# Two token halves of 320 and 320 columns in place of 256 and 384, in contiguous tiles of 640

## The chip, the cores and the metric

The kernel runs on one core of a Trainium2 chip. The metric is the time of one execution on the device, in microseconds (us). The engines are TensorE (matmul; PE in the profile, its weight loads PEld), VectorE (DVE), ScalarE (ACT), GpSimd (POOL) and SyncE (SP, which only issues transfers here). They run side by side, each through its own list of instructions in order, and wait for each other through semaphores.

## The reference, cut to what matters

Two layers of a trunk that works on 640 tokens: 128 of a prompt and 512 of a sample, which have their own modulation vectors.

```python
def _layer(x, cvec, p, ctx):                     # once for the prompt, once for the sample
    sh1, sc1, g1, sh2, sc2, g2 = split(silu(cvec) @ p['ada_w'] + p['ada_b'], 6)
    h = rms(x, p['norm1_g']) * (1 + sc1) + sh1   # over the 1024 features of a token
    sc_b, sc_c, sc_h, q, k, v, dn_qkv, dn_z, dn_a, dn_b = split(h @ p['w_in'])
    y_sc = sc_b * dwconv(sc_c * sc_h)            # short gated convolution
    y_att = attention(q, k, v)                   # windowed, with a cached context for the sample
    y_dn = gated_delta(dn_qkv, dn_z, dn_a, dn_b) # forward and backward scan over chunks
    x = x + g1 * (concat([y_sc, y_att, y_dn]) @ p['w_out'])
    h2 = rms(x, p['norm2_g']) * (1 + sc2) + sh2
    return x + g2 * ((silu(h2 @ p['w_gate']) * (h2 @ p['w_up'])) @ p['w_down'])
```

All inputs are float32. The model has 1024 features (8 tiles of 128) and 2816 hidden ones (22 tiles).

## The kernel before, in words

Activations lie feature-major: a tile has 128 features as partitions and tokens as columns. So that the products keep float32's precision at the speed of the rounded type, every operand is split into a high part (rounded to float32r) and a low part (the exact rest), and a product of a k-tile is three matmuls: high weights by high activations, high by low, low by high (lines 200 to 206 in `fm_product`; weights `whi`, `wlo` are made from `raw` by `split`, lines 173 and 174).

One accumulator in PSUM holds at most 512 columns, so the 640 tokens are taken in two parts, called halves in the names. Before the change part 0 has tokens 0 to 255 (the prompt's 128 and the sample's first 128) and part 1 tokens 256 to 639. Each part of each feature tile is a tile of its own, high and low: `apool` has 16 slots under the tag `a0` (256 columns) and 16 under `a1` (384 columns). The normalised activations (`hhi`, `hlo`), then the mixer's output (`m0h`, `m0l`, `m1h`, `m1l` in the profile, by part), then the second norm's output and so on go through these slots in turn. A slot is given to the next tile when all reads of the tile in it are over. The feed-forward's hidden tiles (`act0h` and so on, tag `act`) are cut in the same way.

The program of a layer:

- `Norm`: for the residual `xt` (8 tiles of 640 tokens), the squares of a tile are added to `acc` by part (`add`, lines 355 to 361); the last tiles to be finished ("late": three of them after w_out, two after w_down) are squared apart (line 374). `stats` sums acc and the late squares over the partitions with matmuls against a column of ones, one column of PSUM per chunk of 128 tokens (lines 379, 381), makes the scale with VectorE (384) and GpSimd (386) and spreads it over the partitions with a matmul against the identity, per chunk (389). `high` scales a tile (VectorE, 418), adds the shift and rounds (ScalarE, 423 to 427), and makes the low part (VectorE, 431, or GpSimd, 425).
- `mixer`: the projections, the short convolution, the DeltaNet (Gram matrices, inverses of triangular blocks, scan) and the attention, in an order written out in `SEQ`. `make_mix` takes the tiles of the mixer's output; `split` and `put_out` fill them by blocks of tokens; `part_out` multiplies tiles 0, 1, 6 and 7 by w_out and adds to the residual.
- w_out for tiles 2 to 5 (`rows`): the last group has four feature tiles (4 to 7), all on part 0 first, then `half(0)` is asked for, then all four on part 1, then `half(1)`.
- Feed-forward in three chunks of hidden tiles. The first two hidden tiles (`lead`) take gate and up on part 0 first, high parts ahead of low ones, then on part 1; the others take gate 0, gate 1, up 0, up 1. w_down follows each chunk; in the first layer the last three feature tiles are again a group, part 0 before part 1, for the norm ahead of the second layer's mixer. There two leading projections read part 0 first.

The order of instructions on each engine is made by a planner when the kernel is built: it simulates the engines with durations of its own and takes what is ready, by program order and a few raised priorities (the weights' splits). TensorE's order therefore depends on when the planner thinks that inputs are ready, and one-column sums stand between products where there was room. Dependencies go by the region of a tile that is read or written; slots go by whole tiles.

## Time and profile before

| what | value |
|---|---|
| median of three runs | 1807.85 us (1805.13 to 1810.63) |
| span of the profiled execution | 1806.5 us, 34244 instructions |
| TensorE busy | 1725.5 us, 96%, 14179 matmuls |
| VectorE busy | 981.2 us, 54% |
| ScalarE busy | 636.2 us, 35% |
| GpSimd busy | 113.2 us, 6% |
| mean granted clock of TensorE | 0.975 of full speed |

The page gives the profiled execution by its span, from the first to the last instruction; the times of the runs hold what lies around it too. "Busy" of TensorE counts a matmul from its start to a modelled end, and matmuls overlap: how fast a stream runs is read from its starts. A row of the timeline has the start in us, the time that it took, the engine, the line, what is written from what, the shapes and the count of instructions merged into it; in brackets stands idle time just before it and what ended it. PEclk is the granted clock of TensorE as a share of 2.4 GHz; it has two levels, 0.5 (1.2 GHz) and 1.

### The profile page before, as it was taken

The page shows a single profiled execution, that of the slowest core. Times are in us where ns is not written, and L with a number is a line of the kernel's source. Part 1 is how long each engine was busy: PE and PEld are TensorE (multiplying, and loading weights), DVE is VectorE, ACT ScalarE, POOL GpSimd, SP SyncE. Part 2 cuts the span into 40 slices and gives each one's busy share as a digit, 9 for nine tenths or more (in the row PEclk, how much of TensorE's full clock was granted, in tenths as well). Part 3 has the DMA queues.
Part 4 walks back from the last instruction along what each step waited for, and adds up shares of the span by engine and source line. Part 5 has one row for each costly group of instructions (what it writes and reads, how often), then busy time and mean ns, then how long its engine had stood idle before and what let it go on. Part 6 is the DMA issues. An engine that isn't in the chain of part 4 may idle for free. (4 is left out here: it accounts for less than half of the span.)

```text
span 1806.5 us, 34244 instructions
## 1 busy us (share of the span) xinstructions
PE 1725.5 (96%) x14179; PEld 1566.9 (87%) x14179; DVE 981.2 (54%) x2324; ACT 636.2 (35%) x1330; POOL 113.2 (6%) x230
## 2 busy tenths in 40 slices
PE   5998999999999999999999879999999999999998
PEld 3887875488999999999988879655899999999998
DVE  3799767666433333333477995777563333333333
ACT  3545244544322122212255442556352212221221
POOL 1111112000000000000012011220010000000000
PEclk7999999999999999999999989999999999999999
DMA  8512234656242222222232222455722222222222
GB/s 287 174 48 68 80 105 126 204 165 227 70 134 78 82 71 80 73 72 78 91 106 72 60 60 77 144 150 161 231 59 71 71 82 70 82 71 73 80 66 75
DMA packets 230025, 188.41 MB, mean 104 GB/s; under 512 B 11566, under 2 KB 206062, under 8 KB 229870
## 3 DMA queue, kind: packets, MB, share of 16 engines
q1 hardware_dynamic: 212992, 170.70, 31.4%
q10 hardware_dynamic: 16878, 15.53, 2.7%
q8 instruction: 111, 1.82, 0.4%
q14 instruction: 44, 0.36, 0.1%
HBM read 168.64 MB, written 17.56 MB: 103 GB/s over the span
## 5 line engine op out<-in xcount | busy, mean ns | idle before, releaser
L173 ACT CAST whi<-raw 128x1024 fp32r<-128x1024 f32 (+2 forms) x191 | 190.2, 996 | 598.9 <-PE pmm L202 271.5
L174 DVE TENSOR_TENSOR wlo<-raw,whi 128x1024 fp32r<-128x1024 f32 (+2 forms) x191 | 220.9, 1158 | 224.3 <-ACT whi L173 223.1
L200 PE MATMUL pmm<-hhi,whi 128*128 128x256 f32 x1008 | 319.0, 317 | 6.6 <-ACT dnp L517 5.3
L203 PE MATMUL pmm<-hhi,wlo 128*128 128x256 f32 x1008 | 317.4, 316 | 7.1 <-DVE wlo L174 7.1
L202 PE MATMUL pmm<-hlo,whi 128*128 128x256 f32 x960 | 301.7, 314 | 0.0
L200 PE MATMUL pmx<-hhi,whi 128*128 128x384 f32 (+1 forms) x688 | 213.0, 310 | 1.0 <-ACT hhi L427 0.7
L203 PE MATMUL pmx<-hhi,wlo 128*128 128x384 f32 (+1 forms) x688 | 212.9, 310 | 0.0
L200 PEld LDWEIGHTS pmm<-hhi,whi 128*128 128x128 f32 x1008 | 195.9, 194 | 11.1 <-ACT dnp L517 6.1
L203 PEld LDWEIGHTS pmm<-hhi,wlo 128*128 128x128 f32 x1008 | 195.7, 194 | 8.4 <-DVE wlo L174 7.7
L202 PE MATMUL pmx<-hlo,whi 128*128 128x256 f32 (+1 forms) x640 | 197.6, 309 | 0.0
L202 PEld LDWEIGHTS pmm<-hlo,whi 128*128 128x128 f32 x960 | 185.7, 193 | 0.7 <-issue 0.4
L200 PEld LDWEIGHTS pmx<-hhi,whi 128*128 128x128 f32 x688 | 130.3, 189 | 2.5 <-ACT hhi L427 1.5
L203 PEld LDWEIGHTS pmx<-hhi,wlo 128*128 128x128 f32 x688 | 130.3, 189 | 0.4 <-issue 0.4
L202 PEld LDWEIGHTS pmx<-hlo,whi 128*128 128x128 f32 x640 | 121.3, 190 | 0.0
L1533 DVE SCALAR_TENSOR_TENSOR av<-sg,pmx 128x256 f32<-128x256 f32 (+1 forms) x88 | 42.9, 488 | 131.8 <-PE pmx L203 123.9
L446 DVE SCALAR_TENSOR_TENSOR xt<-pmx,mod,xt 128x128 f32<-128x128 f32 (+1 forms) x96 | 39.1, 436 | 96.2 <-PE pmx L203 96.0
L446 DVE SCALAR_TENSOR_TENSOR xt<-pmm,mod,xt 128x128 f32<-128x128 f32 (+1 forms) x96 | 39.0, 436 | 91.6 <-PE pmm L203 89.1
L492 PE MATMUL pmm<-wlo,hhi 128*128 128x256 f32 x240 | 69.2, 289 | 0.7 <-DVE wlo L174 0.7
L491 PE MATMUL pmm<-whi,hhi 128*128 128x256 f32 x240 | 69.7, 292 | 0.0
L493 PE MATMUL pmm<-whi,hlo 128*128 128x256 f32 x240 | 69.3, 289 | 0.0
L1524 ACT ACTIVATE th<-pmm 128x256 f32<-128x256 f32 (+1 forms) x88 | 38.2, 434 | 76.7 <-PE pmm L203 70.7
L1526 DVE SCALAR_TENSOR_TENSOR sg<-th,pmm 128x256 f32<-128x256 f32 (+1 forms) x88 | 42.6, 485 | 41.1 <-ACT th L1524 41.1
(450 smaller groups left out, 3798.0 us busy)
## 6 DMA issues: line engine op xcount, KB each, us to landing
adaw<-in_ada_w_dram SPq DMA_DIRECT2D x64, 512.0 KB, 3.9
raw<-in_w_gate_dram SPq DMA_DIRECT2D x44, 512.0 KB, 3.9
raw<-in_w_up_dram SPq DMA_DIRECT2D x44, 512.0 KB, 3.9
raw<-in_w_in_dram SPq DMA_DIRECT2D x36, 512.0 KB, 4.8
araw<-in_ada_w_dram SPq DMA_DIRECT2D x32, 512.0 KB, 5.0
raw<-in_w_down_dram SPq DMA_DIRECT2D x32, 512.0 KB, 4.1
raw<-in_w_down_dram SPq DMA_DIRECT2D x16, 384.0 KB, 3.6
xm<-xscr SPq DMA_DIRECT2D x16, 320.0 KB, 4.9
```

The source lines that it names most:

```text
L173: (hi_eng or A.copy)(hi, src)
L174: (lo_eng or V).tensor_tensor(out=lo, in0=src, in1=hi.bitcast(F32), op=ALU.subtract)
L200: mm(o, lhsT=wh[:, k], rhs=ah, start=k == 0, stop=False)
L202: mm(o, lhsT=wh[:, k], rhs=al, start=False, stop=False)
L203: mm(o, lhsT=wl[:, k], rhs=ah, start=False, stop=not lead and k == n - 1)
L446: V.scalar_tensor_tensor(out=x[:, sl], in0=pt[:, a0:a1], scalar=gate[:, g:g + 1], in1=x[:, sl], op0=ALU.mult, op1=ALU.add)
L491: mm(pt, lhsT=ah[:, ts], rhs=wh[:, k % 4], start=k == 0, stop=False)
L492: mm(pt, lhsT=ah[:, ts], rhs=wl[:, k % 4], start=False, stop=False)
L493: mm(pt, lhsT=al[:, ts], rhs=wh[:, k % 4], start=False, stop=k == 7)
L1524: A.activation(th, pg[:, 0:n], AF.Tanh, scale=0.5)
L1526: V.scalar_tensor_tensor(out=sgs[h], in0=th, scalar=1.0, in1=pg[:, 0:n], op0=ALU.add, op1=ALU.mult)
L1533: V.scalar_tensor_tensor(out=av, in0=sgs[h], scalar=0.5, in1=pu[:, 0:n], op0=ALU.mult, op1=ALU.mult)
```

## The change

The border between the parts moves from token 256 to token 320, so both have 320 columns, and it no longer lies on a multiple of 128. High and low parts become one tile of 640 columns each (class `Act`, tag `a`, 16 slots), of which a part is a slice. What follows from this in the code: products, gate, up and residual pieces have 320 columns (part 0's residual goes in pieces of 128 and 192 columns, since the prompt ends at 128); `Norm.add` squares part by part; `stats` takes its sums in four chunks of 80 tokens per part, and spreads them in four; at the start of the kernel, where the sums come from token-major rows of 128, the border cuts the third block, so three chunks per part. Writers of whole blocks of tokens no longer cut at the border. The rest of the diff takes comments away.

```diff
-HB = ((0, 256), (256, 640))      # the two parts of the tokens that one product takes
-HN = (256, 384)
+HB = ((0, 320), (320, 640))
+HH = 320
...
-    def atiles(pool, tag, name):
-        return tuple(tuple(pool.tile([128, HN[h]], F32R, tag=f"{tag}{h}", name=f"{name}{h}{x}", bufs=16) for x in "hl")
-                     for h in range(2))
+    class Act:
+        def __init__(self, pool, tag, name, bufs=16):
+            self.hi, self.lo = (pool.tile([128, TOK], F32R, tag=tag, name=f"{name}{x}", bufs=bufs) for x in "hl")
+        def __getitem__(self, h):
+            return self.hi[:, HB[h][0]:HB[h][1]], self.lo[:, HB[h][0]:HB[h][1]]
...
-        o = pt[:, 0:HN[h]]
+        o = pt[:, 0:HH]
...
-            a0, a1 = HB[parts[0]][0], HB[parts[-1]][1]
-            sq = self.ft(a1 - a0, "sq")
-            A.activation(sq, self.xt[k][:, a0:a1], AF.Square)
             for h in parts:
-                V.tensor_tensor(out=self.acc[h], in0=self.acc[h], in1=sq[:, HB[h][0] - a0:HB[h][1] - a0], op=ALU.add)
+                sq = self.ft(HH, "sq")
+                A.activation(sq, self.xt[k][:, HB[h][0]:HB[h][1]], AF.Square)
+                V.tensor_tensor(out=self.acc[h], in0=self.acc[h], in1=sq, op=ALU.add)
...
+            if sums is None:
+                chunks = [(0, 80, t, t * 80) for t in range(4)]
+            elif h == 0:
+                chunks = [(0, 128, 0, 0), (0, 128, 1, 128), (0, 64, 2, 256)]
+            else:
+                chunks = [(64, 128, 0, 0), (0, 128, 1, 64), (0, 128, 2, 192)]
...
-                for t in range(nt):
-                    ts = slice(t * 128, (t + 1) * 128)
-                    mm(st[:, t:t + 1], lhsT=self.acc[h][:, ts], rhs=ones_c, start=True, stop=False)
+                for _, p1, t, a0 in chunks:
+                    ts = slice(a0, a0 + p1)
+                    mm(st[0:p1, t:t + 1], lhsT=self.acc[h][:, ts], rhs=ones_c, start=True, stop=False)
                     for sq in sqs:
-                        mm(st[:, t:t + 1], lhsT=sq[:, ts], rhs=ones_c, start=False, stop=sq is sqs[-1])
-                sums = st[:, 0:nt]
+                        mm(st[0:p1, t:t + 1], lhsT=sq[:, ts], rhs=ones_c, start=False, stop=sq is sqs[-1])
+                sums = st[0:np_, 0:nt]
...
-            for t in range(nt):
-                mm(self.bc[h][:, t * 128:(t + 1) * 128], lhsT=y2[:, t:t + 1].to_broadcast([128, 128]), rhs=ident,
-                   start=True, stop=True)
+            for p0, p1, t, a0 in chunks:
+                mm(self.bc[h][:, a0:a0 + p1 - p0], lhsT=y2[p0:p1, t:t + 1].to_broadcast([p1 - p0, 128]),
+                   rhs=ident[p0:p1, p0:p1], start=True, stop=True)
...
-            hi, lo = (apool.tile([128, n], F32R, tag=f"a{h}", name=name) for name in ("hhi", "hlo"))
-            self.out[k][h] = (hi, lo)
+            if self.out[k] is None:
+                self.out[k] = Act(apool, "a", "h")
+            hi, lo = self.out[k][h]
...
-            return ((0, 128, 0), (128, 256, 128))
-        return ((0, 384, 256),)
+            return ((0, 128, 0), (128, HH, 128))
+        return ((0, HH, HH),)
...
+            cs = slice(t0 * 128, (t0 + nt) * 128)
             for hp in range(2):
-                for h, cs, ts in spans(t0 * 128, (t0 + nt) * 128):
-                    hi, lo = mix[6 + hp][h]
-                    split(po[:, hp, ts], hi[:, cs], lo[:, cs])
+                split(po[:, hp, 0:nt * 128], mix[6 + hp].hi[:, cs], mix[6 + hp].lo[:, cs])
...
-                mix[k] = atiles(apool, "a", "m")
+                mix[k] = Act(apool, "a", "m")
             for m in range(2):
-                for h in range(2):
-                    split(ysc[m][:, HB[h][0]:HB[h][1]], mix[m][h][0], mix[m][h][1])
+                split(ysc[m], mix[m].hi, mix[m].lo)
...
             for tag, bufs in (("th", 3), ("sg", SG_BUFS), ("av", 3)):
-                fp.tile([128, HN[1]], F32, tag=tag, name=tag, bufs=bufs)
+                fp.tile([128, HH], F32, tag=tag, name=tag, bufs=bufs)
...
-                    act.append(atiles(fp, "act", "act"))
+                    act.append(Act(fp, "act", "act"))
```

## Rows read from the trace of the kernel before

**Rows 1.** The page: busy us (share of the span), and PEclk in 40 slices.

```profile
PE 1725.5 (96%) x14179; PEld 1566.9 (87%) x14179; DVE 981.2 (54%) x2324; ACT 636.2 (35%) x1330; POOL 113.2 (6%) x230
...
PEclk7999999999999999999999989999999999999999
```

**Rows 2.** Busy us by stretch: length, PE, PEld, DVE, ACT, POOL, PEclk, DMA, GB/s.

```profile
1000.00:1100.00 100.00, 90.29 (x970) 84.19 (x969) 87.83 (x213) 41.62 (x85) 8.13 (x26) 0.91 0.23 67
...
1600.00:1700.00 100.00, 100.00 (x683) 100.00 (x682) 35.62 (x57) 19.48 (x26) 0.00 (x0) 1.00 0.27 78
```

**Rows 3.** Who PE waited for: us in total, times, longest.

```profile
PE pdn L301 <- DMA araw<-in_ada_w_dram: 8.0, 10, 3.4
...
PE pmm L200 <- ACT dnp L517: 5.3, 2, 3.0
```

**Rows 4.** Line 200 alone over the whole span: PE and PEld busy (count).

```profile
0.00:1806.50 1806.50, 849.06 (x2720) 520.21 (x2720) 0.98 0.35 104
```

**Rows 5.** Timeline of PE: streams of 272, 256 and 384 columns, first and last.

```profile
945.89 0.29 PE L491 MATMUL pmm<-zw,hhi 128*128 128x272 f32 x1
...
948.80 0.29 PE L493 MATMUL pmm<-zw,hlo 128*128 128x272 f32 x1
...
1305.89 0.28 PE L200 MATMUL pmm<-m0h,whi 128*128 128x256 f32 x1
...
1308.76 0.28 PE L200 MATMUL pmm<-m0h,whi 128*128 128x256 f32 x1
...
1318.50 0.33 PE L200 MATMUL pmm<-m1h,whi 128*128 128x384 f32 x1
...
1322.66 0.28 PE L200 MATMUL pmm<-hhi,xhi 128*128 128x256 f32 x1
```

**Rows 6.** One-column sums: a burst's start and end; weight loads of 32 and 128 columns.

```profile
1331.45 0.36 PE L379 MATMUL pxo<-ones_c,acc 128*128 128x1 f32 x2
...
1333.24 0.73 PE L206 MATMUL pmx<-hlo,whi 128*128 128x256 f32 x4
...
L278 PEld LDWEIGHTS pdn<-adaw,c 128*32 128x32 f32 x512 | 13.6, 109 | 18.5 <-DMA adaw<-in_ada_w_dram 8.1 <-issue 5.7
...
L381 PEld LDWEIGHTS pxo<-ones_c,sq x80: 186/192/295, 429.1 to 1333.1; 128*128 128x128 f32 x80
```

**Rows 7.** Spreading the scales, line 389: both halves in the timeline; the whole line.

```profile
1316.02 0.71 PE L389 MATMUL pkq<-ident,ny 128*128 128x128 f32 x4
1316.48 0.42 PE L202 MATMUL pmx<-m1l,whi 128*128 128x384 f32 x1
...
1334.56 1.49 PE L389 MATMUL pkq<-ident,ny 128*128 128x128 f32 x6 [0.24 <-POOL ny L386]
...
L389 PE MATMUL pkq<-ident,ny x40: 274/421/582, 13.8 to 1335.6; 128*128 128x128 f32 x40
```

**Rows 8.** Timeline around the second layer's feed-forward start: scaling, and PE's waits.

```profile
1316.76 2.16 DVE L418 SCALAR_TENSOR_TENSOR t<-xt,msc,pkq 128x128 f32<-128x128 f32 x8 [0.21 <-PE pkq L389]
...
1322.25 0.34 DVE L418 SCALAR_TENSOR_TENSOR t<-xt,msc,pkq 128x128 f32<-128x128 f32 x1
...
1324.31 0.39 PE L200 MATMUL pmm<-hhi,xhi 128*128 128x256 f32 x1 [0.19 <-ACT hhi L427]
...
1328.01 0.39 PE L200 MATMUL pmm<-hhi,xhi 128*128 128x256 f32 x1 [0.44 <-ACT hhi L427]
...
1336.09 2.19 DVE L418 SCALAR_TENSOR_TENSOR t<-xt,msc,pkq 128x384 f32<-128x384 f32 x4 [0.77 <-PE pkq L389]
```

**Rows 9.** Busy us behind the second half's sums: first and last of three stretches.

```profile
450.70:457.50 6.80, 6.68 (x31) 6.39 (x31) 4.07 (x9) 2.43 (x5) 1.80 (x2) 0.50 0.00 1
...
1334.80:1338.20 3.40, 3.40 (x18) 3.40 (x18) 2.54 (x6) 1.09 (x4) 0.00 (x0) 0.50 0.00 0
```

**Rows 10.** Timeline of PE at the norm ahead of the second mixer: its wait.

```profile
936.22 0.44 PE L200 MATMUL pmx<-hhi,whi 128*128 128x384 f32 x1 [0.71 <-ACT hhi L427]
```

More of the change, by code (lines that the diff above doesn't have):

```diff
@@ L344, in __init__ @@
             self.bc = [None, None]
-            self.out = [[None, None] for _ in range(KT_)]
+            self.out = [None] * KT_
         def ft(self, n, name):
@@ L353, in add @@
                 for h in parts:
-                    self.acc[h] = self.fp.tile([128, HN[h]], F32, tag=f"acc{h}", name="acc", bufs=1)
+                    self.acc[h] = self.fp.tile([128, HH], F32, tag=f"acc{h}", name="acc", bufs=1)
                     A.activation(self.acc[h], self.xt[k][:, HB[h][0]:HB[h][1]], AF.Square)
                 return
-            a0, a1 = HB[parts[0]][0], HB[parts[-1]][1]
-            sq = self.ft(a1 - a0, "sq")
-            A.activation(sq, self.xt[k][:, a0:a1], AF.Square)
             for h in parts:
-                V.tensor_tensor(out=self.acc[h], in0=self.acc[h], in1=sq[:, HB[h][0] - a0:HB[h][1] - a0], op=ALU.add)
+                sq = self.ft(HH, "sq")
+                A.activation(sq, self.xt[k][:, HB[h][0]:HB[h][1]], AF.Square)
+                V.tensor_tensor(out=self.acc[h], in0=self.acc[h], in1=sq, op=ALU.add)
         def stats(self, h, sums=None):
             b0, b1 = HB[h]
-            n = HN[h]
-            nt = n // 128
+            n = HH
             if h == 0:
                 self.bcp = pkq()
+            if sums is None:
[4 more added lines that the diff above has]
+                chunks = [(64, 128, 0, 0), (0, 128, 1, 64), (0, 128, 2, 192)]
+            nt = len(chunks)
+            np_ = max(c_[1] for c_ in chunks)
             if sums is None:
@@ L399, in half @@
                     self.stats(h)
-            segs = ((1, slice(0, 128)), (0, slice(128, 256))) if h == 0 else ((0, slice(0, n)),)
+            segs = ((1, slice(0, 128)), (0, slice(128, n))) if h == 0 else ((0, slice(0, n)),)
             rests = []
@@ L485, in tm_product @@
         def tm_product(pt, ws, t):
-            h, ts, _ = spans(t * 128, (t + 1) * 128)[0]
+            ts = slice(t * 128, (t + 1) * 128)
             for k in range(KT_):
                 wh, wl = ws[k // 4]
-                ah, al = hs[k][h]
+                ah, al = hs[k].hi, hs[k].lo
                 mm(pt, lhsT=ah[:, ts], rhs=wh[:, k % 4], start=k == 0, stop=False)
@@ L566, in mixer @@
         if first:
-            outs = [[pool()[:, 0:HN[h]] for h in range(2)] for pool in (pmm, pmx)]
+            outs = [[pool()[:, 0:HH] for h in range(2)] for pool in (pmm, pmx)]
             for ks in (range(4), range(4, KT_)):
@@ L999, in short_conv @@
                     fm_product(pt, wc[0], wc[1], hs, h)
-                    A.copy(csb[:, HB[h][0]:HB[h][1]], pt[:, 0:HN[h]])
+                    A.copy(csb[:, HB[h][0]:HB[h][1]], pt[:, 0:HH])
                 yield
@@ L1278, in put_out @@
         def put_out(y, kv_i, t):
+            cs = slice(t * 128, (t + 1) * 128)
             for hp in range(2):
-                h, cs, _ = spans(t * 128, (t + 1) * 128)[0]
-                hi, lo = mix[2 + kv_i * 2 + hp][h]
-                split(y[:, hp * 128:hp * 128 + 128], hi[:, cs], lo[:, cs])
+                m = mix[2 + kv_i * 2 + hp]
+                split(y[:, hp * 128:hp * 128 + 128], m.hi[:, cs], m.lo[:, cs])
         def values(t, kv_i, P):
@@ L1438, in hybrid_trunk_kernel @@
         norm = Norm(fp, xt, lambda *ks: mod_scale(0, 0, *ks), mods[0][:, 0:8], ())
-        norm.stats(0, sums[:, 0:2])
+        norm.stats(0, sums[:, 0:3])
         norm.stats(1, sums[:, 2:NT])
@@ L1515, in ffn_load @@
                     drain(gen, 1)
[L1516 removed]
+                    act.append(Act(fp, "act", "act"))
                     return g_, u_, {}, act[-1]
                 def gate_half(gw, sgs, h, lead=False):
[L1520 removed]
+                    n = HH
                     pg = pmm()
@@ L1528, in up_half @@
                 def up_half(uw, sgs, at, h, lead=False):
-                    n = HN[h]
+                    n = HH
                     pu = pmx()
```

14 lines of the change are left out of this document (5 added, 9 removed).

## The prediction

> **What bounds the kernel now.** I began with the page: which engine is busy, and in which slices. TensorE is busy 96% of the span, VectorE 54%, and the granted clock is at its upper level, 2.4 GHz, in nearly every slice [rows 1]. The busy times by stretch say where this holds: in the feed-forward part TensorE is busy 100.00 us of 100 and starts 683 matmuls in them; in the mixer it is busy 90.29 of 100 at a mean clock of 0.91, with VectorE at 87.83 [rows 2]. Then the list of who waited for whom: TensorE's waits are small and spread; the longest are for weights of the first stage (8.0 us) and for the copy out of a projection's accumulator (5.3 us in two waits) [rows 3]. So the bound is the stream of matmuls on TensorE, and the change is priced by what it does to that stream and to the few places where the stream waits.
>
> **Part 1: the columns of the products.** Every feature-major product (k-tile by k-tile: high, low, high) runs once per half. Line 200 stands in the trace 2720 times [rows 4]; each k-tile has three such matmuls, so there are 3 x 2720 = 8160, half of them with 256 and half with 384 columns. The change keeps the count and the sum of columns and gives each 320. That is worth nothing if time from start to start is a straight line in the columns. The starts in the timeline say [rows 5]: 24 matmuls of 256 columns take 1308.76 - 1305.89 = 2.87 us, 119.6 ns each; 24 of 384 take 1322.66 - 1318.50 = 4.16 us, 173.3 ns; 23 of 272 take 2.91 us, 126.5 ns. From 256 to 384 the slope is 53.7 / 128 = 0.42 ns a column, one column per cycle of 2.4 GHz, and the line through them gives 126.3 at 272 (measured 126.5). So 256 is not held up by something else (a weight load that takes longer than the columns), and 320 should take (119.6 + 173.3) / 2 = 146.5 ns. Term: 0. It is the one with the largest lever: half a nanosecond per matmul off the line is 8160 x 0.5 = 4.1 us, either way. No run here shows 320 columns.
>
> **Part 2: the sums of squares.** The three norms that follow a residual sum over the partitions with one-column matmuls, per chunk of tokens. Chunks go from 2 + 3 of 128 tokens to 4 + 4 of 80. Each fp32 matmul is two instructions, so a chunk has 2 x (1 + late tiles): (5 chunks x 8) x 2 + 5 x 6 = 110 before, (8 x 8) x 2 + 8 x 6 = 176 after. In the burst of 16 from 1331.45 to 1333.24 one takes 1.79 / 16 = 112 ns [rows 6]: one column of work, so this is its weight load. Are 80 weight columns cheaper than 128? A load of 32 columns has a mean of 109 ns, one of 128 a median of 192 [rows 6], 0.86 ns a column, so 48 columns fewer make 112 - 41 = 71 ns. Then 176 x 71 = 12.5 us against 110 x 112 = 12.3: +0.2. The other end is that each instruction keeps its 112 ns: 66 x 112 = +7.4. I take +0.2, by the two loads of different widths. The Trainium skill (TensorE: Matmul & The Clock Gate, section LDWEIGHTS) has a load take its columns divided by 1.2, in ns, whatever the rows: an estimate by it is 66.7 ns for 80 columns, and 66.7 x 176 against 106.7 x 110 comes to +0.0; the trace's two widths agree with it in slope (0.86 against 0.83 ns a column).
>
> **Part 3: spreading the scales.** Line 389 goes from 40 instructions to 60 [rows 7]: 18 of the 20 new ones in the three norms, 2 at the start, where TensorE waits for weights anyway [rows 3]. The stationary operand stays 128 columns wide. Four take 1316.48 - 1316.02 = 0.46 us, 115 ns each; in the second half of a norm six run at the lower clock, 1.2 GHz [rows 9], and take (1.49 - 0.42) / 5 = 214 ns from start to start, with the median duration of one for the last [rows 7]. Half 0 gets four more (0.46), half 1 two more (0.43): 0.9 per norm, +2.7 in all. Bounds: 0 (if they go by the sum of their moving columns, which stays 640) and 3.8 (all 18 at 214).
>
> **Part 4: half 0 of a norm.** While TensorE runs the last four tiles of w_out on half 1, VectorE and ScalarE normalise half 0, and the feed-forward's first products, on half 0, come next. This cover is 4 x 12 matmuls, and it shrinks by 48 x 26.8 = 1.29 us; meanwhile half 0 grows. VectorE's pieces of 128 take 2.16 / 8 = 0.27 us, of 384 2.19 / 4 = 0.55 [rows 8], 1.1 ns a column; 64 columns more on 8 scalings and 5 low parts are 13 x 0.07 = 0.9. Half 0 falls behind TensorE by 2.2 us. There is little slack: the scaling of tile 4 starts at 1322.25, 0.4 before the products on half 0 begin at 1322.66, and TensorE already waits twice for a high part (0.19 and 0.44) [rows 5, 8]. But the consumer slows as well: the 64 matmuls of the four leading products on the high parts take 64 x 26.9 = 1.7 longer. Left: +0.5 per such norm. At the norm before the second mixer the cover is 3 x 18 matmuls (1.45 less) and only 32 follow (0.86): 1.45 + 0.9 - 0.86 = +1.5. Sum +2.5; bounds 0 and 2 x 2.2 + 2.35 = 6.8.
>
> **Part 5: half 1 of a norm.** The reverse: 0.9 us less work, and more cover. In the feed-forward TensorE did not wait there. Before the second mixer it waited 0.71 us for a high part [rows 10]; the two products in front take 48 x 26.9 = 1.3 longer now. Term -0.7; bounds -2.2 and 0.
>
> **Part 6: the writers.** One 640-column tile saves splits where a block crossed the border (two of the short convolution, two of the DeltaNet's output per layer): 8 pairs, and on VectorE the fixed part of an instruction is 0.27 - 128 x 1.1 / 1000 = 0.13, so 1.0 us. Ten squares of 640 columns become twenty. VectorE and ScalarE are not the bound and TensorE's stream covers both: 0, and -1.0 if the mixer's share of them ends a wait.
>
> **The sum.** 0 + 0.2 + 2.7 + 2.5 - 0.7 = +4.7 us on the span of 1806.5, that is 1811.2. The page gives the profiled execution by its span alone; the median of the runs, 1807.85, lies 1.35 above it. So 1812.5; I write 1812.
>
> **The rivals.** First, slower: the tiles' slots. The old tags let half 0's tiles go when half 0 was read; now the 16 slots hold both halves, and eight of them (mix 2 to 5, high and low) are read until the end of the last products on half 1. Whoever writes half 0 of the normalised tiles there must wait for that end. It decides from the point where more than the four free pairs are needed before it: today tile 4 comes 0.4 us before that end [rows 8], so a wait costs little; if the slots go round in order instead and tiles 2 to 7 or all eight wait, then at the (1328.01 - 1322.25) / 4 = 1.4 us of a tile [rows 8] the last high part is there after 8 x 1.4 = 11.2 us, its last 8 matmuls take 1.2, and the 64 would have taken 64 x 0.1465 = 9.4: 3 us late, twice, less the 1 counted above, is +5: 1817. For it: the slots are full. Against: four pairs are free early.
>
> Second, slower: the clock. Behind each second half's sums the granted clock stood at 1.2 GHz, in three stretches, of 6.8, 3.4 and 3.4 us [rows 9]; what went before was a burst of one-column matmuls [rows 6] and a wait for the scales. Half 0's burst doubles from 16 to 32 instructions. One more stretch of 3.4 us per norm costs half of it, 1.7: 3 x 1.7 = 5.1, 1817. The Trainium skill (TensorE: Matmul & The Clock Gate, Part 1, What's actually happening) has the lower clock as the default that activity lifts, which speaks against more sparse matmuls.
>
> Third, faster: with longer products ahead of half 1 those three stretches go (13.6 us at half speed, 6.8 back), and so does the 5.3 us wait for the accumulator's copy [rows 3], since no product lasts only 24 x 119.6 ns any more: 1812 - 12 = 1800.
>
> Fourth: 320 columns are off the line by half a nanosecond: 1808 or 1816.
>
> **How the numbers follow.** My forecast, 1808 to 1816: 0.46. Slots, 1814 to 1820: 0.20. Clock, 1814 to 1820: 0.11. Faster, 1798 to 1803: 0.12. Off the line: 0.11, 0.03 of it faster by enough, 0.04 slower. A measurement of this kernel tells about 0.3% from no change, 5.4 us: 1802.4 to 1813.3. The forecast lies near the upper edge and gives 0.12 of its share to slower. Faster 0.09 + 0.03 = 0.12; slower 0.12 + 0.17 + 0.09 + 0.04 = 0.42; same 0.46. The range 1802 to 1822 leaves out the faster case and the sum of two slower ones.
>
> **What would show it.** Starts of 320-column matmuls 146 to 147 ns apart and 683 in 100 us of feed-forward: part 1. One-column matmuls 71 ns apart: part 2. Waits of TensorE for a high part near the start of the feed-forward up by half a microsecond: part 4; by 3: the slots. A stretch at 1.2 GHz behind the sums of half 0: the clock. The forecast is wrong if 320 columns take under 146 or over 147 ns, or if the mixer, whose order is laid out anew around the new durations, moves by more than the norms do.

## The result, and the profile of the changed kernel

The changed kernel is slower: 1828.57 us (median of four, 1823.29 to 1831.92) against 1806.62 in the same comparison, a ratio of 1.0108 with a 95% interval of 1.0080 to 1.0135. The forecast was 1812, its range 1802 to 1822. The profiled execution spans 1827.6 us, 21.1 more than the one of before.

First, of the changed kernel, the page's busy times and clock (before: [rows 1]), a stretch of the feed-forward part ([rows 2]), and the starts of two products twelve matmuls apart in the timeline of PE ([rows 5]).

```profile
PE 1737.6 (95%) x14265; PEld 1573.5 (86%) x14265; DVE 977.7 (53%) x2316; ACT 636.0 (35%) x1332; POOL 112.9 (6%) x230
...
PEclk7998999998999999999999999899999999999999
...
1600.00:1700.00 100.00, 100.00 (x684) 100.00 (x683) 35.74 (x57) 19.55 (x27) 0.00 (x0) 1.00 0.26 76
...
1323.18 0.31 PE L199 MATMUL pmm<-mh,whi 128*128 128x320 f32 x1
...
1324.94 0.31 PE L199 MATMUL pmx<-mh,whi 128*128 128x320 f32 x1
```

The bulk of the work costs what it did: 1.76 us for twelve is 146.7 ns each, and 684 matmuls start in 100 us where 683 did. So the 21 us lie elsewhere. To find them I cut both traces at the same events: the last product of the attention's values in a mixer, the ninth tanh of the feed-forward behind it, that feed-forward's last tanh, the second mixer's first z product, its first scan product. A stretch that is called a norm below thus holds the rest of the output projection (or of w_down), the norm and the first products behind it. Busy us by stretch (length, PE, PEld, DVE, ACT, POOL, PEclk, DMA, GB/s), of the kernel before:

```profile
0.00:409.30 409.30, 364.99 (x3682) 286.45 (x3682) 288.01 (x813) 191.30 (x460) 49.27 (x111) 0.94 0.45 140
409.30:512.80 103.50, 102.57 (x722) 96.15 (x719) 54.97 (x114) 37.56 (x75) 7.60 (x8) 0.97 0.45 142
512.80:873.10 360.30, 360.30 (x2482) 357.77 (x2481) 128.38 (x204) 81.00 (x122) 0.00 (x0) 1.00 0.28 80
873.10:945.90 72.80, 70.49 (x468) 68.08 (x467) 44.37 (x94) 31.11 (x63) 7.44 (x15) 0.98 0.33 102
945.90:1079.70 133.80, 120.19 (x1152) 109.08 (x1151) 115.61 (x303) 64.88 (x130) 16.33 (x40) 0.92 0.24 68
1079.70:1292.70 213.00, 201.69 (x2251) 147.88 (x2251) 145.41 (x441) 100.25 (x273) 24.95 (x48) 0.99 0.47 145
1292.70:1388.50 95.80, 94.23 (x638) 92.46 (x635) 55.05 (x111) 37.56 (x73) 7.59 (x8) 0.98 0.30 89
```

and of the changed kernel:

```profile
0.00:411.20 411.20, 365.05 (x3681) 285.86 (x3683) 288.33 (x809) 190.40 (x456) 49.01 (x111) 0.95 0.44 139
411.20:523.00 111.80, 108.36 (x753) 101.27 (x750) 53.46 (x114) 38.50 (x77) 7.54 (x8) 0.94 0.42 134
523.00:883.00 360.00, 360.00 (x2480) 357.66 (x2479) 128.54 (x204) 81.01 (x122) 0.00 (x0) 1.00 0.27 80
883.00:958.50 75.50, 72.13 (x492) 69.35 (x490) 43.79 (x94) 31.59 (x65) 7.85 (x15) 0.98 0.32 98
958.50:1087.80 129.30, 117.10 (x1151) 106.34 (x1151) 114.94 (x304) 65.03 (x132) 16.13 (x40) 0.96 0.25 70
1087.80:1310.60 222.80, 207.69 (x2248) 150.16 (x2249) 145.86 (x438) 98.88 (x269) 24.83 (x48) 0.96 0.44 139
1310.60:1410.70 100.10, 96.92 (x671) 94.17 (x668) 53.18 (x111) 38.16 (x76) 7.54 (x8) 0.98 0.28 85
```

Row by row: the first mixer +1.9, layer 0's norm ahead of the feed-forward +8.3, the feed-forward -0.3, the norm ahead of the second mixer +2.7, the second mixer -4.5 and +9.8, layer 1's norm +4.3. The three norms carry 15.3 of the 21, the mixers 7.2; the rest, behind the last row, is 1.0 shorter. Each of these figures is from one execution. Then who waited (PE: us in total, times, longest), first the row of the kernel before for the wait in question, then the changed kernel:

```profile
PE pkq L389 <- POOL ny L386: 1.0, 3, 0.5
...
PE pdn L300 <- DMA araw<-in_ada_w_dram: 7.2, 8, 2.3
...
PE pkq L395 <- POOL ny L392: 6.4, 7, 1.4
...
PE pmm L199 <- ACT dnp L524: 3.6, 2, 2.1
```

The wait for `ny`, the scales, is 6.4 us in seven pieces: the longest, 1.4, stands at 15 us in the kernel's first stage, the other six, 5.0 in all, at both halves of the three norms. In the kernel before the row is 1.0 in three, all in the norms. The two waits of [rows 3] did not grow; one for other weights of the first stage, `adaw`, did, from 6.3 to 8.3. Now the place of such a wait, the timeline at layer 0's half 0: before,

```profile
431.43 0.81 PE L381 MATMUL pxo<-ones_c,sq 128*128 128x1 f32 x6
432.10 0.42 PE L202 MATMUL pmm<-m1l,whi 128*128 128x384 f32 x1
...
432.58 0.70 POOL L386 TENSOR_TENSOR ny<-nms,mhalf 128x2 f32<-128x2 f32 x1 [101.03 <-DVE nms L384]
...
433.34 0.71 PE L389 MATMUL pkq<-ident,ny 128*128 128x128 f32 x4
```

and after:

```profile
438.11 0.24 PE L387 MATMUL pxo<-ones_c,sq 128*80 128x1 f32 x2
...
439.93 0.39 PE L202 MATMUL pmx<-mh,wlo 128*128 128x320 f32 x1
440.10 0.16 DVE L390 TENSOR_SCALAR nms<-pxo 80x4 f32<-80x4 f32 x1 [1.98 <-PE pxo L387]
440.15 0.31 PE L199 MATMUL pmx<-mh,whi 128*128 128x320 f32 x1
440.30 0.31 PE L201 MATMUL pmx<-ml,whi 128*128 128x320 f32 x1
440.40 1.02 POOL L392 TENSOR_TENSOR ny<-nms,mhalf 80x4 f32<-80x4 f32 x1 [108.27 <-DVE nms L390]
441.48 2.00 PE L395 MATMUL pkq<-ident,ny 80*128 80x80 f32 x8 [0.86 <-POOL ny L392]
443.20 0.61 PE L202 MATMUL pmx<-mh,wlo 128*128 128x320 f32 x1
```

From the end of the sums to the first product that spreads the scales it is 1.24 us before and 1.55 after. Before, six products of 384 columns stand between and fill that time; after, three of 320 (0.44 us), and TensorE stands for the other 1.1 (0.86 of it in the row; ends of matmuls are modelled). Behind it the granted clock is at its lower level: the eight spreading instructions take 1.72 us, 215 ns each against 115 [rows 7]. The stretches at the lower clock that answer to [rows 9] there and at the norm ahead of the second mixer:

```profile
441.30:448.10 6.80, 6.62 (x26) 6.63 (x27) 4.35 (x12) 2.90 (x6) 1.14 (x2) 0.50 0.03 8
465.20:468.60 3.40, 3.40 (x15) 3.40 (x15) 3.17 (x8) 2.34 (x5) 0.87 (x1) 0.50 0.02 5
929.40:932.80 3.40, 3.40 (x15) 3.40 (x14) 3.10 (x7) 2.83 (x6) 0.00 (x0) 0.50 0.01 2
```

Not all of layer 0's +8.3 belongs to this place. Earlier in the stretch TensorE waits for the mixer's output, and the clock is at the lower level from 417.4 to 420.8; in the kernel before the longest such wait is 0.31 us, with no such fall:

```profile
415.93 0.42 PE L199 MATMUL pmm<-mh,whi 128*128 128x320 f32 x1 [1.46 <-ACT mh L172]
```

### The profile page after: what moved, and what is told of

It is laid out like the page before. It is cut to its first block, busy times and chain, and to the rows that moved or that the text cites. A ratio compares the mean times of both kernels' runs of the same rounds, so it can differ in the third digit from the quotient of the medians.

```text
span 1827.6 us, 34398 instructions
## 1 busy us (share of the span) xinstructions
PE 1737.6 (95%) x14265; PEld 1573.5 (86%) x14265; DVE 977.7 (53%) x2316; ACT 636.0 (35%) x1332; POOL 112.9 (6%) x230
## 5 line engine op out<-in xcount | busy, mean ns | idle before, releaser
L199 PE MATMUL pmm<-hh,whi 128*128 128x320 f32 x1008 | 319.6, 317 | 6.4 <-ACT dnp L524 3.6
L202 PE MATMUL pmm<-hh,wlo 128*128 128x320 f32 x1008 | 318.5, 316 | 6.6 <-DVE wlo L173 6.5
L201 PE MATMUL pmm<-hl,whi 128*128 128x320 f32 x960 | 300.8, 313 | 0.0
L199 PE MATMUL pmx<-hh,whi 128*128 128x320 f32 x688 | 212.5, 310 | 0.2 <-ACT hh L431 0.2
L202 PE MATMUL pmx<-hh,wlo 128*128 128x320 f32 x688 | 212.2, 309 | 0.0
L199 PEld LDWEIGHTS pmm<-hh,whi 128*128 128x128 f32 x1008 | 193.6, 192 | 11.7 <-ACT dnp L524 4.5
L202 PEld LDWEIGHTS pmm<-hh,wlo 128*128 128x128 f32 x1008 | 193.2, 192 | 8.7 <-DVE wlo L173 7.4
L201 PE MATMUL pmx<-hl,whi 128*128 128x320 f32 x640 | 197.9, 309 | 0.0
L201 PEld LDWEIGHTS pmm<-hl,whi 128*128 128x128 f32 x960 | 182.8, 190 | 0.3
L199 PEld LDWEIGHTS pmx<-hh,whi 128*128 128x128 f32 x688 | 129.2, 188 | 0.9 <-ACT hh L431 0.4
L201 PE MATMUL pmx<-actl,whi 128*128 128x320 f32 x340 | 105.5, 310 | 0.0
```

Source lines behind the costliest of these rows:

```text
L199: mm(o, lhsT=wh[:, k], rhs=ah, start=k == 0, stop=False)
L201: mm(o, lhsT=wh[:, k], rhs=al, start=False, stop=False)
L202: mm(o, lhsT=wl[:, k], rhs=ah, start=False, stop=not lead and k == n - 1)
```

## The experiments

The suspects were: A, the border with what hangs on it in the norms (squares by halves, 80-column sums, addresses, the longer half 0); B, the slots of the contiguous tiles; C, an order of the instructions that was laid out anew; and, from the timelines, P, the place of the spreading products. Ratios are against the kernel before, with 95% intervals.

**Which part of the change.** `e1_layout` is the kernel before with the contiguous tiles alone:

```
-        return tuple(tuple(pool.tile([128, HN[h]], F32R, tag=f"{tag}{h}", ...
+            self.hi, self.lo = (pool.tile([128, TOK], F32R, tag=tag, ...
```

> The layout alone: activations in contiguous 640-column tiles from one set of 16 slots, the border between the token halves back at 256 as in the kernel before, with its 128-column sums of squares, its one square of 640 columns and its 384-column th, sg and av slots. Theory A (the loss comes from the border, through the norms and the slots of th, sg and av that shrank with it): within 0.3% of the kernel before, 1803 to 1812 us. Theory B (slots: a 640-column slot comes free later than a 256-column one, and w_out's last products hold it): the start of the first FFN waits for the high part of the norm, some 3 us per layer more, 1810 to 1814 us. Theory C (the order of the second mixer, laid out anew around any change, is what moves): the order on the engines differs from the kernel before already here, and the scan and attention of layer 1 move by several us either way: any time from 1800 to 1830 us, with the norms of layer 0 (scales of its second norm at 433 us) where they were.

Measured: 1.0025 (1.0006 to 1.0044), the stretches of the norms at 104.3, 72.4 and 95.6 us, where the kernel before has 103.5, 72.8 and 95.8. So the layout costs something by itself, 0.25%, but not in the norms: the slots are not the main loss.

`e2_border_ffn` and `e3_border_mixer` set the border by stage: BM for the mixers, BF from the output projection to the end of the feed-forward. The first has

```
+BM, BF, PRE = 256, 320, 320
...
     for l in range(depth):
         gen = ada(l, 2, 6, wraw)
+        border(BM)
...
+            border(BF)
             last_layer = l == depth - 1
```

and the second the same with `BM, BF, PRE = 320, 256, 384` (PRE is the width of the th, sg and av slots).

> Contiguous tiles everywhere; the border is at 320 from each layer's output projection to the end of its FFN (with the norms that are computed there) and at 256 in the norm of the input and in both mixers; the th, sg and av slots are 320 columns wide as in the changed kernel. Theory A (border in norms and FFN, with the slots that shrank): nearly the whole loss is here, 1822 to 1830 us, the loads of xt in layer 0 stand at 414 to 421 us as in the changed kernel. Theory B (slots of the contiguous tiles) the same as the layout alone. Theory C (order of the mixers): the loss of layer 1's mixer, 8 to 10 us of the 21, goes or stays by chance of the new order; the 6 to 9 us at layer 0's output projection stay: 1812 to 1830 us.

> Contiguous tiles everywhere; the border is at 320 in the norm of the input and in both mixers, and at 256 from each layer's output projection to the end of its FFN, with the norms computed there; th, sg and av slots 384 columns wide as in the kernel before. Theory A: within 0.3% of the kernel before (the changed parts of the norms and the slots are not in it), 1803 to 1812 us, xt loads of layer 0 at 410 to 416 us. Theory C (the mixers' order): layer 1's scan and attention carry the 8 to 10 us that they lose in the changed kernel, 1814 to 1818 us.

Measured: 1.0122 (1.0099 to 1.0145) and 1.0071 (1.0044 to 1.0097). The border between the output projection and the end of the feed-forward alone loses as much as the whole change. e3 is above theory A's 0.3% too, and the two losses do not add up to the changed kernel's. In e3 the norm ahead of the second mixer takes 81.0 us instead of 72.8, with a wait of 5.2 us for the second half's added squares in it, which no other kernel's trace has there: the mixer's first 320 columns need 64 of the norm's second half. That is a price of mixing borders, and little else can be read from e3's time.

`e4_slots384` gives xt its old addresses:

```
-                fp.tile([128, HH], F32, tag=tag, name=tag, bufs=bufs)
+                fp.tile([128, 384], F32, tag=tag, name=tag, bufs=bufs)
```

> The changed kernel with one edit: the slots for th, sg and av are 384 columns wide again (their tiles still 320), so that xt's tiles lie at the addresses that they have in the kernel before. The order of the instructions on every engine is that of the changed kernel; addresses, and the waits that follow from them, are all that differs. Theory A1 (part of the loss is that xt's tiles, at addresses lower by the shrunken slots, lie over mixer tiles that are released later, so that their loads, which stand in ScalarE's queue, come late and hold up what is behind them): the loads of xt go back to 410 to 416 us, the stretch from 411 to 442 us is 5 to 9 us shorter, 1819 to 1824 us. Theory C (the order alone): nothing moves, 1824 to 1833 us.

Measured: 1.0114 (1.0079 to 1.0148), as the changed kernel. The eight loads of xt are issued within 8.2 us instead of 10.3, and layer 0's norm takes 110.6 us instead of 111.8: at most 1.2 us, not theory A1's 5 to 9. Its order of instructions is the changed kernel's, so it also shows how well a stretch repeats: layer 1's norm takes 100.1 us in both.

**Which property of 320.** Three edits of e2_border_ffn, and a border of 384:

```
-                chunks = [(0, 80, t, t * 80) for t in range(4)]
+                chunks = [(0, 128, 0, 0), (0, 128, 1, 128), (64, 128, 2, 256)]
```

is `e5_three_sums`; one square over both halves, as in the kernel before, is `e6_one_square`; `e8_both_undone` has both; `e7_border_384` has `BF = 384` with the old sums and squares.

> The kernel of e2_border_ffn (border 320 from the output projection to the end of the FFN, 256 in the mixers) with one edit: the sums of squares of a half in three chunks of up to 128 columns instead of four of 80, and the scales spread by three products instead of four. Compared with e2_border_ffn (1.0122). Theory H (the length of the halves: half 0 takes longer to normalise and half 1 covers it for a shorter time): within 0.3% of e2_border_ffn, 1826 to 1835 us. Theory S (more one-column products and spreading products between the residual and the norm): 5 us or more of the 22 come back, 1815 to 1825 us.

> The kernel of e2_border_ffn with one edit: the squares of a feature tile are taken for all 640 columns at once, as in the kernel before, where the changed kernel takes them half by half (ten squares more on ScalarE; VectorE's sums stay two per tile). Theory H: within 0.3% of e2_border_ffn, 1826 to 1835 us. Theory Q (the squares by halves fill ScalarE's queue in front of the splits of weights that the products want): 5 us or more come back, 1815 to 1825 us.

> Contiguous tiles, border 256 in the mixers, and 384 from the output projection to the end of the FFN: halves of 384 and 256 columns, so the same two shapes of products, the same 128-column sums, the same square of 640 columns and the same slots as in e1_layout, with the longer half first. Theory H: the loss grows with half 0: from 256 to 320 columns it was 18 us (e2_border_ffn less e1_layout), so about as much again, 1840 to 1855 us. Theories S and Q (the 80-column sums, or the squares by halves): neither is in this kernel, so it stands by e1_layout, 1808 to 1818 us.

> The kernel of e2_border_ffn with the edits of e5_three_sums and e6_one_square together: of the changed norm only the border of 320 is left. Theory H: within 0.3% of e2_border_ffn, 1826 to 1835 us. Theories S and Q: by e1_layout, 1810 to 1818 us, even if each edit alone gave less.

Measured: 1.0099 (1.0070 to 1.0128), 1.0068 (1.0044 to 1.0091), 1.0035 (1.0009 to 1.0060) and 1.0063 (1.0041 to 1.0086). A longer half 0 is not it: e7 has the longest and loses least of these, so theory H falls. The sums alone bring nothing that can be told from e2. One square (e6), and both edits together (e8), lie clear of e2's interval: one square seemed to bring 10 us. But e6's norms ahead of the feed-forwards still took 107.2 and 100.2 us; what the edit had moved showed only later (e10, e18).

**The order around the split.** In the changed kernel VectorE's low part of a weight split (1.23 us) stands in front of the last residual of half 0; before, it stood behind. `e9_pin` puts the split behind the squares, `e10_pin_square` adds the one square, `e11_both_pin` does it to e8, `e12_before_pin` to the kernel before:

```
+                    tc.add_manual_dep(casts[-1].ins, late.ins.name, NOSYNC, reason="behind the squares")
```

> The changed kernel with one order pinned, at the norm ahead of each FFN: the split of the fourth FFN weight (its high part on ScalarE, its low part on VectorE) stands behind the squares of half 0's late feature tiles, where the changed kernel has it ahead of the last tile's residual and square. No computation is added or left out. Theory O (order: the split, 1.05 us on ScalarE and 1.23 us on VectorE, holds up the last square, so the scales of half 0 come late, TensorE stands 1.9 us before the products that spread them, and its clock falls): at 438 to 446 us and at 1335 to 1340 us the wait for the scales is under 0.5 us, and 2 to 4 us come back at each of the two norms, 1819 to 1825 us. Theory N (320 columns cost it by themselves, through longer squares, residuals and sums): under 2 us in all, 1826 to 1832 us.

> The changed kernel with the pinned order of e9_pin and with the squares of a feature tile taken for all 640 columns at once, as in e6_one_square. Theory O with the squares by halves as a second cause (e6_one_square took 0.54% off): both come back, 1809 to 1816 us, within 0.5% of the kernel before. Theory N: only the squares' part comes back, 1817 to 1824 us.

> The kernel of e8_both_undone (border 320 from the output projection to the end of the FFN, 256 in the mixers, three sums a half, one square of 640 columns) with the pinned order of e9_pin. Theory O: what e8_both_undone loses against e1_layout, some 7 us, is the place of the split, and this kernel stands by e1_layout, 1809 to 1815 us, with no wait of TensorE for a square at 1320 to 1324 us. Theory N: by e8_both_undone, 1816 to 1824 us.

> The kernel before with the pinned order of e9_pin. There the split stands ahead of the last square on ScalarE too, but behind the last residual on VectorE. Theory O: the last square of half 0 comes up to 1 us earlier at two norms, so 0 to 3 us faster, 1803 to 1808 us; if it is more than 2 us slower, the order of these few instructions alone does not carry the loss, and the split that now comes late costs as much elsewhere.

Measured: 1.0096 (1.0066 to 1.0126), 1.0112 (1.0097 to 1.0128), 1.0080 (1.0056 to 1.0104), and for the kernel before a loss, 1.0050 (1.0035 to 1.0065). Theory O falls as it was put: in e9 the sums of layer 0 end 3.7 us behind half 0's last product instead of 4.9, yet the wait behind them is the same 0.86 us, and its time cannot be told from the changed kernel's. e10, at 1829 us, is above what either theory gave it; e11 is where theory N had it. And e12 lost 9 us by an edit that theory O had at 0 to 3 us faster. Its timeline shows a wait that the kernel before does not have:

```profile
431.08 0.42 PE L203 MATMUL pmm<-m1l,whi 128*128 128x384 f32 x1
...
431.34 1.23 DVE L174 TENSOR_TENSOR xlo<-raw,xhi 128x1024 fp32r<-128x1024 f32 x1
...
431.56 1.57 POOL L389 TENSOR_TENSOR ny<-nms,mhalf 128x2 f32<-128x2 f32 x1 [100.21 <-DVE nms L387]
433.18 0.71 PE L392 MATMUL pkq<-ident,ny 128*128 128x128 f32 x4 [1.32 <-POOL ny L389]
```

With the split gone from in front of `nms`, the planner had put the spreading products behind three products instead of six. The way over VectorE and GpSimd, 1.24 us in the kernel before and 2.10 here, is then no longer covered. That the planner takes this way for shorter than it is would fit its choice; no run shows what it takes it for.

**The place of the spreading products.** `e13_spread_later` (the changed kernel) and `e14_ffn_spread` (e2_border_ffn) hold them back by a dependency in the order alone, `e15_before_spread` does it to the kernel before; `e16_mixer1_256` has the border at 256 in the second mixer only.

```
+    def behind(nrm, h, product):
+        for ins in nrm.spread[h]:
+            tc.add_manual_dep(ins.ins, product.ins.name, NOSYNC, reason="scales later")
...
+                    if last and h:
+                        behind(nrm, 0, prods[at + (28 if nk == 4 else 20)])
```

> The changed kernel with one order pinned: in the norm ahead of each FFN and the norm ahead of the second mixer, the products that spread the scales stand 10 to 12 products behind the last sum of squares (6 at one place), where the changed kernel has 3 at all six places. No computation is added or left out. Theory P (placement: from the end of the sums to the scales it takes 1.5 us, three products of 147 ns cover 0.44 of it, TensorE stands for the rest, and the clock falls behind it): the wait for the scales, 6.4 us in seven pieces, falls under 1.5 us, the norms' half-clock stretches at 441, 465 and 929 us go, and 5 to 10 us come back, 1818 to 1824 us. Theory N (the sizes of squares, sums and residuals set when the scaled tiles are there, so that the wait only moves to the first products of the next stage): within 3 us of the changed kernel, 1825 to 1832 us.

> The kernel of e2_border_ffn (border 320 from the output projection to the end of the FFN, 256 in the mixers; 1.0122) with the pinned order of e13_spread_later. Theory P: without the second mixer's part of the loss too, so it comes nearest to the kernel before, 1812 to 1820 us. Theory N: as e2_border_ffn, 1825 to 1833 us.

> The kernel before with the same order pinned: the spreading products stand 10 products behind the last sum at half 0 and 4 to 8 at half 1, where it has 6, 3 and 6 at half 0 and 4, 4 and 7 at half 1. Theory P: at 915 us the wait of 0.5 us goes, the others are covered already, so 0 to 3 us faster, 1803 to 1808 us. Theory C (any new order of these engines costs some us against the one that the kernel before has): 2 to 10 us slower, 1809 to 1817 us, as e12_before_pin was by 9 us.

> The changed kernel with the border back at 256 in the second mixer alone (norms, first mixer and FFN at 320). Theory M (the border in that mixer sets an order in which TensorE's clock falls four times between its scan and the end of its attention, 17 us at half clock against 3): that stretch is 5 to 9 us shorter and its first part 3 to 5 us longer, as in e2_border_ffn, in all 2 to 5 us faster than the changed kernel, 1823 to 1827 us. Theory D (those falls follow from where the work stands in time after the norms): no change, 1826 to 1832 us.

Measured: 1.0050 (1.0031 to 1.0068), 1.0052 (1.0029 to 1.0074), 0.9996 (0.9978 to 1.0015) and 1.0145 (1.0116 to 1.0174). Theory P holds in the time of e13: the changed kernel's interval begins at 1.0080, e13's ends at 1.0068. In the same way e2's begins at 1.0099 and e14's ends at 1.0074. Of e13, the norms' stretches, the wait, and the timeline at the place shown above:

```profile
414.50:517.40 102.90, 100.90 (x753) 95.04 (x750) 54.80 (x114) 38.26 (x78) 8.00 (x8) 1.00 0.46 145
...
877.30:952.50 75.20, 72.27 (x493) 70.36 (x491) 44.94 (x94) 31.64 (x66) 7.89 (x15) 0.95 0.33 100
...
1303.20:1399.40 96.20, 94.34 (x671) 92.61 (x668) 54.44 (x111) 37.96 (x76) 7.99 (x8) 1.00 0.29 89
...
PE pkq L400 <- POOL ny L397: 1.8, 2, 1.4
...
441.68 0.39 PE L202 MATMUL pmx<-mh,wlo 128*128 128x320 f32 x1
...
442.16 1.01 POOL L397 TENSOR_TENSOR ny<-nms,mhalf 80x4 f32<-80x4 f32 x1 [108.36 <-DVE nms L395]
...
443.51 1.01 PE L400 MATMUL pkq<-ident,ny 80*128 80x80 f32 x8
```

GpSimd takes its 1.01 us as ever; TensorE runs twelve products meanwhile, and the clock stays at 1.00 through both norms ahead of a feed-forward. They are at 102.9 and 96.2 us, where the changed kernel had 111.8 and 100.1 and the kernel before 103.5 and 95.8. Of the wait, 1.4 of the 1.8 us is the piece in the first stage; 0.4 is left in the norms. Theory P missed in the norm ahead of the second mixer, where the clock still fell (0.95 in its row), and in e14, which came no nearer to the kernel before than e13. In layer 0, part of the gain, the shorter wait for the mixer's output (0.75 us) and no fall of the clock behind it, is not the place's: e4, in the changed kernel's order, has 0.84 us and no fall there either. From the changed kernel to e13 the order differs only around the three norms, but there not in the spreading products alone: 45 of VectorE's 2316 instructions and 50 of ScalarE's 1332 stand elsewhere too. e15 says that a new order is not a loss by itself, and that the kernel before had nothing left to gain here. In e16 the second mixer's two stretches are 132.9 and 216.9 us, 3.6 longer and 5.9 shorter than the changed kernel's, as theory M had it, but the time of the whole, 1837 us, is above what either theory gave it; the execution that was profiled, 1828 us, is the shortest of its five. What the border does in that mixer thus stays open.

**The reverse, and the squares once more.** `e17_before_early` puts half 0's spreading products of the kernel before where the changed kernel has them; `e18_spread_square` adds the one square to e14.

```
+                tc.add_manual_dep(product.ins, ins.ins.name, NOSYNC, reason="scales first")
```

> The kernel before with one order pinned: in the norm ahead of each FFN, half 0's products that spread the scales stand 3 products behind the last sum of squares (in layer 0 with four adaLN products besides), where it has 6. No computation is added or left out. Theory P (the place does the harm): at about 1333 us before, now in front of the first spreading product of half 0 in layer 1, TensorE waits 0.7 to 1 us for the scales where it waited 0.2, the clock may fall behind it, and the norm ahead of layer 1's FFN gets 1 to 5 us longer; layer 0's, with the four products as cover, 0 to 3 us; 1808 to 1816 us in all. Theory N: within 0.2% of the kernel before, 1803 to 1811 us.

> The kernel of e14_ffn_spread with one square of 640 columns per feature tile, as in the kernel before (e6_one_square's edit). Theory Q (the squares by halves carry what e14_ffn_spread still loses, 0.5%): 1810 to 1815 us, by e1_layout. Theory R (with the scales in place, the squares cost nothing; e6_one_square had moved the spreading products from 3 to 4 or 6 behind the last sum): within 3 us of e14_ffn_spread, 1816 to 1824 us.

Measured: 1.0029 (1.0012 to 1.0046) and 1.0049 (1.0028 to 1.0070). e17 has nothing of the change but the place, and what the planner laid out anew behind it, and loses; in layer 1:

```profile
1322.71 0.42 PE L202 MATMUL pmm<-m1l,whi 128*128 128x384 f32 x1
...
1323.95 0.71 PE L395 MATMUL pkq<-ident,ny 128*128 128x128 f32 x4 [0.47 <-POOL ny L392]
...
1300.50:1401.50 101.00, 97.59 (x639) 95.50 (x636) 54.38 (x111) 37.11 (x74) 6.86 (x8) 0.95 0.28 85
```

That norm takes 101.0 us instead of 95.8, 5.2 more where 1 to 5 were forecast, but the wait for half 0's scales is 0.47 of it, less than was forecast. Later in the stretch TensorE waits 1.16 us for a normalised tile and 0.72 for half 1's added squares, behind an order of VectorE that is new too, and from there the clock is at the lower level for 10.2 us instead of 3.4, which costs 3.4. So e17 shows what the early place brings about in this kernel, not what the wait alone costs. In layer 0, with eight adaLN instructions as cover besides the three products, the norm takes 105.2 instead of 103.5. e18 equals e14, so the squares by halves cost nothing once the scales are in place: theory Q falls, R holds.

All kernels side by side: products between the last sum of half 0 and the first spreading product, counted in the traces of PE, and the length of the two norms' stretches.

| kernel | layer 0: products, us | layer 1: products, us |
|---|---|---|
| before | 6, 103.5 | 6, 95.8 |
| e1 | 6, 104.3 | 6, 95.6 |
| e3 | 6, 105.0 | 6, 95.3 |
| e7 | 6, 106.2 | 6, 97.0 |
| e13 | 12, 102.9 | 12, 96.2 |
| e14 | 12, 104.1 | 12, 96.3 |
| e15 | 10, 103.0 | 10, 96.6 |
| e18 | 15, 104.3 | 15, 96.5 |
| changed | 3, 111.8 | 3, 100.1 |
| e2 | 3, 111.7 | 3, 101.7 |
| e4 | 3, 110.6 | 3, 100.1 |
| e5 | 3, 107.2 | 3, 105.5 |
| e6 | 4, 107.2 | 4, 100.2 |
| e8 | 4, 105.9 | 4, 106.8 |
| e9 | 3, 108.5 | 3, 99.0 |
| e10 | 3, 107.9 | 3, 101.6 |
| e11 | 3, 107.9 | 3, 99.8 |
| e12 | 3, 105.5 | 3, 101.7 |
| e16 | 3, 111.6 | 3, 100.0 |
| e17 | 3 and 8 adaLN, 105.2 | 3, 101.0 |

In layer 1 every kernel with six or more is at 97.0 us or below and every one with three or four at 99.0 or above, whatever its border, sums and squares; the sum of both layers splits as cleanly, 203.2 at most against 206.2 at least. Layer 0 by itself does not: e7's 106.2 lies above e12, e17 and e8. The table counts half 0 alone and does not say that the place made every figure in it. In e8's layer 1 TensorE waited 1.8 us for the last square and not for half 0's scales, and the clock had fallen before them; in e12's it waited 3.3 us for normalised tiles besides. How far above a kernel lies varies with where the clock falls.

## Why the prediction was wrong, step by step

- **Part 1 was right.** 146.5 ns forecast, 146.7 measured; layer 0's feed-forward stretch changed by 0.3 us.
- **Part 2 was right in its count and its price**: the traces have 110 and 176 such instructions in the norms, and the 26 from 438.11 to 439.93 take 70 ns each (71 forecast).
- **Part 3 is the step that failed.** It priced the spreading products by their count, +2.7 with 3.8 as its upper end, and took for granted that what stands in front of them would go on covering the chain from the sums to the scales. In the changed kernel this wait took 5.0 us in the three norms instead of 1.0, with the lower clock behind it at four of the six places; e13, with the place mended, gets 0.58% of the 1.08% back, about 10 of the 20 us. That half is shown by experiment; what is left lies in no part of the sum (see the caution below). The chain itself grew by 0.3 us, since GpSimd's power over four columns takes 1.02 us instead of 0.70 over two; its cover shrank from 1.0 us to 0.44. The prediction's own rows held the warning: four instructions behind a covered wait, six behind one of 0.24 [rows 7].
- **Parts 4 and 5 were about right.** With the place mended (e13) the three norms take 102.9 + 75.2 + 96.2 = 274.3 us against 272.1 before: +2.2 for Parts 2 to 5 together, where the sum had +4.7. That this is less is luck: the clock is at the lower level for 6.8 us of them instead of 13.6 and so gives back 3.4, which no part of the sum had; without it they are at +5.6. Nearer to what the two parts are about: TensorE's waits for a normalised tile in the three norms are 2.0 us before and 4.2 in e13, +2.2 where they had 2.5 - 0.7 = +1.8.
- **Part 6's zero for the squares held** (e18); that it looked otherwise in e6 goes with the place, which the edit had moved from 3 to 4 products at half 0 and to 6 at half 1 ahead of the feed-forwards. No run measures the splits that it saves.
- **The rivals.** Slots: not in the norms, where e1 is as the kernel before, though the layout's 0.25% has no account here. The clock: right in kind, smaller in size. The time at 1.2 GHz in the three norms' stretches went from 13.6 us [rows 9] to 13.7 + 3.4 + 3.4 = 20.5, which costs half the difference, 3.4 us, where the rival had 5.1; and 3.4 of the 20.5, the fall at 417.4, stands behind the wait for the mixer's output and not behind the sums. With the wait for the scales gone (e13) the clock stayed up in the two norms ahead of a feed-forward, so there it looks like a follower of the wait; in the norm ahead of the second mixer it fell for 6.8 us all the same. The faster case and 320 off its line: neither.
- **The caution at the end** (wrong if the mixers, laid out anew, move by more than the norms) did not come true in size, but a third of the loss in the profiled execution is there: 1.9 and 5.3 us. In the second mixer's second stretch TensorE is at the lower clock for 17.1 us instead of 3.4 (6.8 us lost) and stands 15.1 us instead of 11.3. e14, with the border at 256 there, has a clock of 0.99 in it; but its ratio is that of e13, and e16's is no better than the changed kernel's. The first mixer also differs by 8.4 us between two executions with the same order on every engine (the changed kernel, 411.2, and e4, 419.6): the lower clock, for 44.4 and 61.4 us, makes up all of it. All twenty traces together say a little more. The first mixer takes 411.2 to 419.6 us (mean 414.2) in the seven kernels with the border at 320 there and 406.5 to 412.7 (409.1) in the thirteen with 256; the second takes 350.3 to 354.6 (352.3) in six and 346.2 to 352.0 (349.4) in fourteen. By the means, the border in the mixers goes with some 8 us. But the kernels with 256 there are not faster by so much (e2 against the changed kernel, e14 against e13), so this part is not settled, and neither is its cause.

What is left in e13, 0.5%, lies in its trace in the first mixer (+5.2 us), the norm ahead of the second mixer (+2.4) and the second mixer (+3.9); the 0.25% that e1 loses with the layout alone is in the same 0.5%, and no run divides it further. No kernel here beats the one before: e15 equals it.

## What to carry to other kernels

A chain that hops from TensorE over two engines and back has a latency, and it is the work that stands ahead of the returning instruction in TensorE's queue that hides it: count that work in us on both sides of a change, not the instructions in the chain. Where a planner sets the order, a change of sizes changes such counts in places that no line of the diff names; compare the order around every return to the busiest engine, and hold it with a dependency where the planner leaves too little in front. And before a single edit is believed (e6, e17), see what else it moved in the order.

## What the runs showed of the hardware

- GpSimd's power on a few columns takes 0.70 us for 2 and 0.85 for 3 columns of 128 rows (the kernel before) and 1.01 for 4 columns of 80 rows (the changed kernel): 0.15 a column on top of 0.4, by these three. In e12, with VectorE's 1.23 us subtraction of two SBUF tiles beside it, the one on 2 columns took 1.57. The Trainium skill (GPSIMD Engine Reference, section 1, Specifications) has GpSimd's SBUF interfaces shared with VectorE, with contention where VectorE reads two SBUF inputs; this row agrees.
- TensorE's matmuls did not pass a waiting one: in the rows above each spreading product starts behind just the products that stand ahead of it in the program, and those behind it start after it, however long it waits. The Trainium skill (TensorE: Matmul & The Clock Gate, Part 2, Step-by-step: what each phase is for) states that order for matmuls, and the traces agree; hence the place in the queue decides.
- TensorE standing for 1.1 us behind a burst of one-column matmuls went with 6.8 us at the 1.2 GHz level in layer 0 (from 441.3) and with none in layer 1, where the same sequence ran in the changed kernel at 1335 us and its eight spreading instructions took 0.91 us instead of 1.72; the price of one wait thus varies by some 3 us between places that look alike.
